# Moving z products, merge gates and the first scan in the order of a four-block fp32 kernel

## The chip, the cores and the metric

One core of one Trainium2 chip. The metric is the device time of one execution in microseconds. The times before are 3188.27, 3188.68 and 3191.09 us, median 3188.68.

## The reference

Two layers of a first block (retention, two convolution branches, a gated feed-forward part), then two layers of a second block, on 512 positions of width 1024 in float32. The change touches the second block alone. Cut to that:

```python
h = rmsnorm_2(x, pre_norm_g[l]); proj = h @ w_in[l]
u, v, z_a, c_q, c_kv, k_rope, z_b, x_c, z_c, g_a, g_b, g_c = split(proj)
y_a = gmlp_spatial(u, v, ...) * silu(z_a)
y_b = mla_attention(c_q, c_kv, k_rope, ...) * silu(z_b)      # 8 heads, softmax(q k^T) v
y_c = rg_lru(x_c, ...) * silu(z_c)                           # width 1280
merged = sigmoid(g_a) * (y_a @ w_proj_a[l]) + sigmoid(g_b) * (y_b @ w_proj_b[l]) \
       + sigmoid(g_c) * (y_c @ w_proj_c[l])
x = x + rmsnorm_2(merged @ w_out[l], post_norm_g[l])

# rg_lru: causal convolution of 4 taps, then
r = sigmoid(xb @ w_a + b_a); i = sigmoid(xb @ w_x + b_x)     # blocks of 80 channels
a = exp(-8 * r * softplus(-lam)); b = sqrt(max(1 - a * a, 0)) * (i * xc)
h[t] = a[t] * h[t-1] + b[t]                                  # the scan over positions
```

## The kernel before

Every large product is made in three passes: an operand x is split into a part that the fast fp32r format holds, hi (on ScalarE, lines 179, 307, 315), and the rest, lo = x - hi (on VectorE, lines 180, 308, 316), and `mm3` (lines 323 to 325) issues hi x hi, hi x lo and lo x hi. Channels lie on the 128 partitions, the 512 positions along the free dimension. A projection of 128 output channels from 1024 inputs (`projT`) is 8 blocks, so 24 matmuls of 512 columns.

The weights come from memory in one long stream, laid out in the order in which the program takes them. `Stream` loads them in pairs of chunks (1 MB, line 166, on SyncE's queue, two buffers), and splits a chunk of 1024 columns, 8 blocks, into hi and lo when the program comes within `AHEAD` = 4 chunks of it; `RING` = 7 split chunks fit. The split is issued at that point of the program, on ScalarE (line 179) and VectorE (line 180), so it stands in their queues behind all that was issued earlier.

The program is one hand-written order: each engine runs its instructions in the order in which the code issues them, and waits for the others by semaphores. Work that may be spread is put into a lane, a generator; `tick` runs one step of each lane, and `drain` the rest.

The second block (`block2`) runs `mla_down`, three z products of the B branch, the attention (`mla`), the merge of B, the recurrence (`lru`), the merge of C, the gMLP branch, the merge of A and the output projection. A z product is a `projT`, a sigmoid on ScalarE (line 942) and a product on VectorE (line 943).

In `mla`, `group(0)` makes the rotated parts of four heads' queries, then z(3), then head 0's projections and their split (`proj_split`, lines 315 and 316). For each head come the scores (from line 998), the next head's projections, the normalisation of the probabilities on VectorE (line 1016), then fillers from the table `FILL`: v a group of values, p the product with the values of the head before (`pv`, line 1048), g the second group of rotations, z a z product. At the end `out` transposes the probabilities on TensorE (line 1027). After head 7: z(7), then pv(7). In `merge` (B with two, C with four gates ahead) a gate is a `projT` and a sigmoid (line 673); output m is a product with all operands (line 684).

In `lru` there are ten tiles of 128 channels. A loop over m issues conv(m + 3), copies of rows between tiles by DMA (`pack`), a z product of C at m = 4, 6, 7, 8, and gates(m) (sigmoids line 1175, product line 1178). A scan (`scan`, a lane) is: two exponentials per tile on ScalarE (lines 1188, 1189), a small step on VectorE (line 1191), the square roots (line 1194), then per tile a product and the scan (lines 1197, 1198). The first scan has tiles 0 to 3 and is issued after gates(3), with two ticks per tile; it is drained before the second, of tiles 4 to 9, is issued behind the loop. A second loop issues the other six z products and, between them, multiplies finished operands (line 1239) and splits them, lo on POOL. The last two operands come behind that loop (line 1249).

Of the kernel before, what the change touches and what calls it, by code (L numbers as in the profile page):

```python
# [23 lines left out]
RING = 7  # L24
# [61 lines left out]
ZPOS = (4, 6, 7, 8)  # L86


FILL = ("v", "p", "gp", "p", "pv", "zp", "zp", "zp")
UNITS = 16  # L90


# [145 lines left out]
class Kernel:  # L238
# [709 lines left out]
    def mla(self, l, c, zb):  # L948

        nc, s, p = self.nc, self.s, self.p  # L950
# [5 lines left out]
        def group(g):  # L956
            pa = self.projT("mla_w_uq_2", l, ("qr", g, 0), op=c["cq"])
            pb = self.projT("mla_w_uq_2", l, ("qr", g, 1), op=c["cq"])
            x1, x2 = self.rotate(pa, pb, c["cos"], c["sin"])
            for i in range(4):  # L960
                grp["q", 4 * g + i] = self.stack(i, (x1.hi, x2.hi, x1.lo, x2.lo))
            return x1.hi, x1.lo, x2.hi, x2.lo
# [99 lines left out]
        def z(h):  # L1062

            t = self.z_silu(l, E_ZB + 128 * h)
            if h < len(zb):
                nc.vector.tensor_tensor(zb[h][:], zb[h][:], t[:], op=ALU.mult)
                s.f(t)
            else:
                zb.append(t)

        used = group(0)
        z(3)
        proj_split(0, *proj(0))
        for h in range(8):
            self.ws.ahead(self.ws.cur + AHEAD + 1)
            scores(h)
# [16 lines left out]
        s.f(c["cos"], c["sin"], c["kr"].hi, c["kr"].lo)  # L1093
        for o in c["cq"] + c["ckv"]:
            s.f(o.hi, o.lo)
        z(7)
        pv(7)
        for h in range(4):
            zb[h] = self.split(zb[h])

    def lru(self, l):
        nc, s, p = self.nc, self.s, self.p
        tt = nc.vector.tensor_tensor
        xc, op = {}, {}
        ws = self.ws

        lam = self.col("lam", l, 0, NLT)
        sp = self.sm.tile([128, 6 * NLT], F32, tag="sp", name="sp", bufs=1)
        a, b, c, d, sc1, sc2 = (sp[:, NLT * i:NLT * i + NLT] for i in range(6))
        ts = nc.vector.tensor_scalar  # L1110
        ts(a, lam, -1.0, 0.0, op0=ALU.mult, op1=ALU.max)
        ts(b, lam, 0.0, 2.0, op0=ALU.max, op1=ALU.mult)
        tt(b, lam, b, op=ALU.subtract)
        nc.scalar.activation(c, b, AF.Exp)
        nc.scalar.activation(d, c, AF.Ln, bias=1.0)
        tt(a, a, d, op=ALU.add)
        ts(sc1, a, -8.0, None, op0=ALU.mult)
        ts(sc2, a, -16.0, None, op0=ALU.mult)

        def conv(m):  # L1120
            ps = self.projT("w_in_2", l, E_XC + 128 * m)
            w = lambda k: self.col("lcw", l, 4 * m + k)
            t = s.t()
            nc.scalar.activation(t[:], ps[:], AF.Identity, bias=self.col("lcb", l, m), scale=w(3))
            for k in (2, 1, 0):
                sh = 3 - k
                nc.vector.scalar_tensor_tensor(t[:, sh:], ps[:, :S - sh], w(k), t[:, sh:], op0=ALU.mult, op1=ALU.add)
            p.f(ps)
            hi, lo = s.t(F32R), s.t(F32R)
            nc.scalar.activation(hi[:], t[:], AF.Copy)  # L1130
            tt(lo[:], t[:], hi.r(), op=ALU.subtract)
            xc[m], op[m] = t, Op(hi, lo)
            self.tick()

        rr, ii, pk = {}, {}, {}

        def pack(m):

            out = lru_outside(m)
            n = sum(r1 - r0 for _, r0, r1 in out)  # L1140
            one = 3 * n <= 128
            tiles = [s.t(F32R)] if one else [s.t(F32R), s.t(F32R)]
            for i, part in enumerate(("hi", "lo", "hi") if one else ("hi", "lo")):
                t, o = (tiles[0], n * i) if one else (tiles[i], 0)
                for k, r0, r1 in out:
                    eng = nc.sync if part == "lo" else nc.gpsimd
                    eng.dma_start(t[o:o + r1 - r0, :].bitcast(F32), getattr(op[k], part)[r0:r1, :].bitcast(F32))
                    o += r1 - r0
            pk[m] = (n, tiles)

        gw = {}

        def gate_weights(m):

            n = len(lru_rows(m))
            for nm in ("lru_w_a_2", "lru_w_x_2"):
                a = ws.take(128, (nm, l, 128 * m, 128 * m))
                hi, lo = ws.take(128, (nm, l, lru_rows(m), 128 * m))
                if n % 3 == 0 and n <= 96:
                    k = slice(n // 3 * 2, n)  # L1160
                    nc.gpsimd.tensor_copy(hi[k], lo[k].bitcast(F32))
                gw[nm, m] = (a, (hi, lo))

        def gates(m):
            n, tiles = pk.pop(m)
            for nm, bias, dst in (("lru_w_a_2", "lba", rr), ("lru_w_x_2", "lbx", ii)):
                a, (hi, lo) = gw.pop((nm, m))
                ps = p.t()
                self.mm3(ps[:], a, (op[m].hi[:], op[m].lo[:]), True, False)
                if len(tiles) == 1:  # L1170
                    nc.tensor.matmul(ps[:], hi[0:3 * n], tiles[0][0:3 * n, :], start=False, stop=True)
                else:
                    self.mm3(ps[:], (hi[0:n], lo[0:n]), (tiles[0][0:n, :], tiles[1][0:n, :]), False, True)
                t = s.t()
                nc.scalar.activation(t[:], ps[:], AF.Sigmoid, bias=self.col(bias, l, m))
                p.f(ps)
                dst[m] = t
            tt(ii[m][:], ii[m][:], xc[m][:], op=ALU.mult)
            o = op.pop(m)
            s.f(xc.pop(m), o.hi, o.lo, *tiles)  # L1180
            self.tick()

        h = {}

        def scan(ms):
            for m in ms:
                h[m] = s.t()
                nc.scalar.activation(h[m][:], rr[m][:], AF.Exp, scale=sc2[:, m:m + 1])  # L1188
                nc.scalar.activation(rr[m][:], rr[m][:], AF.Exp, scale=sc1[:, m:m + 1])  # L1189
            for m in ms:  # L1190
                ts(h[m][:], h[m][:], 1.0, 0.0, op0=ALU.subtract, op1=ALU.min)
            yield
            for m in ms:
                nc.scalar.activation(h[m][:], h[m][:], AF.Sqrt, scale=-1.0)  # L1194
            yield
            for m in ms:
                tt(ii[m][:], ii[m][:], h[m][:], op=ALU.mult)  # L1197
                nc.vector.tensor_tensor_scan(h[m][:], rr[m][:], ii[m][:], 0.0, op0=ALU.mult, op1=ALU.add)
                s.f(rr.pop(m), ii.pop(m))
                yield  # L1200
                if len(ms) == 4:
                    yield

        conv(0)
        conv(1)
        pack(0)
        conv(2)
        pack(1)
        pz, sz = {}, {}
        gate_weights(0)  # L1210
        for m in range(NLT):
            if m + 1 < NLT:
                gate_weights(m + 1)
            if m + 3 < NLT:
                conv(m + 3)
                pack(m + 2)
                if m + 3 == NLT - 1:
                    pack(NLT - 1)
            if m in ZPOS:
                z = len(sz) + len(pz)  # L1220
                ps = self.projT("w_in_2", l, E_ZC + 128 * z)
                if m < 8:
                    sz[z] = self.silu(ps)
                else:
                    pz[z] = ps
                self.tick()
            gates(m)
            if m == 3:
                self.lane("scan", scan(range(4)))
        self.drain("scan")  # L1230
        self.lane("scan", scan(range(4, NLT)))
        ops = []
        nz = len(sz) + len(pz)
        for z in range(nz, NLT):
            pz[z] = self.projT("w_in_2", l, E_ZC + 128 * z)
            self.tick()
            for m in range(len(ops), z - 1):
                t = sz.pop(m) if m in sz else self.silu(pz.pop(m))
                tt(t[:], t[:], h[m][:], op=ALU.mult)  # L1239
                s.f(h.pop(m))  # L1240
                ops.append(self.split(t, eng=nc.gpsimd))
                if m >= nz - 2:
                    break
            self.tick()
        self.drain("scan")
        rest = [self.silu(pz.pop(m)) for m in range(len(ops), NLT)]
        for t in rest:
            m = len(ops)
            tt(t[:], t[:], h[m][:], op=ALU.mult)
            s.f(h.pop(m))  # L1250
            ops.append(self.split(t))
        return ops
# [69 lines left out]
    def block2(self, l, last=False):  # L1322
        s = self.s
        c = self.mla_down(l)
        zb = []
# [5 lines left out]
            if h:  # L1331
                self.tick(3)
        self.drain("mla")
        self.mla(l, c, zb)

        def yb():
            return [z if isinstance(z, Op) else self.split(z) for z in zb]

        acc = {}
# [166 lines left out]
```

## Time and profile before

| | us |
|---|---|
| median of three runs | 3188.68 |
| the profiled execution | 3187.51 |
| its span, first to last instruction | 3185.7 |
| TensorE busy (mean granted clock 0.999) | 3139.7 (99%) |
| VectorE busy | 1862.8 (58%) |
| ScalarE busy | 1192.0 (37%) |
| POOL busy | 236.0 (7%) |

PE is TensorE, PEld its weight load, DVE VectorE, ACT ScalarE, SP SyncE. In a timeline a row has the start (us from the span's start), the length, the engine, the line, the operation, out<-in by the program's names without numbers (s a slot in SBUF, p a bank in PSUM, whi and wlo the split weights, hh and hl the split input), the shape and how many in a row; in brackets the engine's idle time ahead of it and what ended that. Matmuls overlap, so their pace is read from start to start. In the rows on stretches: the stretch and its length, the busy time of PE, PEld, DVE, ACT and POOL with (x instructions), the granted clock of TensorE, the share of the DMA engines, GB/s. The four blocks follow each other; the second block's two layers repeat the same pattern about 771 us apart (TensorE at 2057.09 and 2828.53).

### The profile page before, as it was taken

Reading aid. Unit: us, or ns where it says so; the run is one execution under the profiler, and the core shown is the slowest. Engines: PE = TensorE matmul, PEld = TensorE weight load, DVE = VectorE, ACT = ScalarE, POOL = GpSimd, SP = SyncE. Lnnn points to the kernel's source line nnn. Section 1 sums busy time; section 2 is a strip of 40 time slices with the busy share of each in tenths; the row PEclk is TensorE's granted clock in tenths of the full one; section 3 lists DMA queues with packets and bytes.
Section 4 is the critical chain, followed back from the end, with each engine's and each line's share of the span. In section 5 each row is a group of like instructions: output and inputs, shape, how many; then the busy total and the mean of one; then the engine's idle time right before and its main releaser. Section 6 shows DMA issues by size and latency. Waiting matters only on the chain. (4 is left out here: it accounts for less than half of the span.)

```text
span 3185.7 us, 36912 instructions
## 1 busy us (share of the span) xinstructions
PE 3139.7 (99%) x14808; PEld 2637.0 (83%) x14808; DVE 1862.8 (58%) x2727; ACT 1192.0 (37%) x1798; POOL 236.0 (7%) x364
## 2 busy tenths in 40 slices
PE   8999999999999999999999999999999999999998
PEld 7888888888888888888888888788888888878887
DVE  5687556663568755666448636735546854663643
ACT  4222343343322233333345525622225543642222
POOL 2000010000200000000011001200002000120000
PEclk9999999999999999999999999999999999999999
DMA  6222322232432232223323123332333223332232
GB/s 197 93 100 93 132 80 106 93 119 106 146 106 87 93 132 83 103 93 108 117 85 126 54 105 113 126 126 80 119 119 119 79 80 105 118 126 106 93 106 73
DMA packets 62539, 337.98 MB, mean 106 GB/s; under 512 B 10304, under 2 KB 10432, under 8 KB 27552
## 3 DMA queue, kind: packets, MB, share of 16 engines
q1 hardware_dynamic: 49984, 302.54, 26.8%
q0 software_dynamic: 11232, 31.08, 3.4%
q8 instruction: 116, 1.90, 0.2%
q10 hardware_dynamic: 1152, 2.01, 0.2%
q14 instruction: 55, 0.45, 0.0%
HBM read 310.68 MB, written 8.39 MB: 100 GB/s over the span
## 5 line engine op out<-in xcount | busy, mean ns | idle before, releaser
L323 PE MATMUL p<-hh,whi 128*128 128x512 f32 (+1 forms) x2752 | 1048.8, 381 | 1.6 <-ACT whi L179 1.6
L325 PE MATMUL p<-hh,wlo 128*128 128x512 f32 (+1 forms) x2752 | 1045.2, 380 | 1.5 <-DVE wlo L180 1.5
L324 PE MATMUL p<-hl,whi 128*128 128x512 f32 (+1 forms) x2752 | 1045.0, 380 | 0.0
L180 DVE TENSOR_TENSOR wlo<-raw,whi 128x1024 fp32r<-128x1024 f32 x544 | 671.7, 1242 | 476.7 <-ACT whi L179 475.5
L179 ACT ACTIVATE whi<-raw 128x1024 fp32r<-128x1024 f32 x544 | 563.2, 1052 | 313.5 <-PE p L325 189.1
L325 PEld LDWEIGHTS p<-hh,wlo 128*128 128x128 f32 x2752 | 518.6, 188 | 99.3 <-DVE wlo L180 1.8
L323 PEld LDWEIGHTS p<-hh,whi 128*128 128x128 f32 x2752 | 518.9, 189 | 98.5 <-ACT whi L179 2.0
L324 PEld LDWEIGHTS p<-hl,whi 128*128 128x128 f32 x2752 | 519.0, 189 | 96.1
L323 PE MATMUL p<-s,whi 128*128 128x512 f32 (+1 forms) x768 | 300.2, 391 | 3.1 <-ACT whi L179 2.6
L325 PE MATMUL p<-s,wlo 128*128 128x512 f32 (+1 forms) x768 | 299.2, 390 | 1.0 <-DVE wlo L180 1.0
L324 PE MATMUL p<-s,whi 128*128 128x512 f32 (+1 forms) x768 | 299.4, 390 | 0.4 <-DMA s<-s 0.4
L323 PE MATMUL p<-whi,s 128*128 128x512 f32 x640 | 250.1, 391 | 0.0
L325 PE MATMUL p<-whi,s 128*128 128x512 f32 x640 | 249.2, 389 | 0.0
L324 PE MATMUL p<-wlo,s 128*128 128x512 f32 x640 | 249.1, 389 | 0.0
L307 ACT ACTIVATE s<-s 128x512 fp32r<-128x512 f32 x168 | 103.4, 627 | 361.1 <-DVE s L689 129.4
L673 ACT ACTIVATE s<-p 128x512 f32<-128x512 f32 x96 | 57.3, 597 | 414.4 <-PE p L325 414.4
L813 DVE SCALAR_TENSOR_TENSOR s<-p,pv,s 128x511 f32<-128x511 f32 (+1 forms) x176 | 131.8, 749 | 122.3 <-ACT s L810 119.2
L684 DVE TENSOR_TENSOR s<-p,s 128x512 f32<-128x512 f32 x96 | 66.3, 690 | 194.2 <-PE p L325 194.2
L567 DVE SCALAR_TENSOR_TENSOR s<-s,pv,s 128x511 f32<-128x511 f32 (+14 forms) x240 | 176.0, 733 | 5.7
L323 PEld LDWEIGHTS p<-s,whi 128*128 128x128 f32 (+1 forms) x768 | 144.3, 188 | 34.1 <-ACT whi L179 3.5
L325 PEld LDWEIGHTS p<-s,wlo 128*128 128x128 f32 (+1 forms) x768 | 144.1, 188 | 32.0 <-DVE wlo L180 1.9
L324 PEld LDWEIGHTS p<-s,whi 128*128 128x128 f32 (+1 forms) x768 | 144.3, 188 | 30.3 <-DMA s<-s 0.5
(187 smaller groups left out, 3046.4 us busy)
## 6 DMA issues: line engine op xcount, KB each, us to landing
raw<-in_w_dram SPq DMA_DIRECT2D x272, 1024.0 KB, 4.8
s<-in_rows_dram POOLq DMA_DIRECT2D x32, 256.0 KB, 3.5
s<-s POOLq DMA_DIRECT2D x96, 64.0 KB, 2.6
xd<-s SPq DMA_DIRECT2D x24, 256.0 KB, 2.0
s<-xd POOLq DMA_DIRECT2D x24, 256.0 KB, 3.3
s<-s SPq DMA_DIRECT2D x88, 64.0 KB, 2.8
s<-in_cst_dram POOLq DMA_DIRECT2D x16, 256.0 KB, 3.6
s<-in_x_dram POOLq DMA_DIRECT2D x8, 256.0 KB, 5.5
```

The costliest lines, as they stand in the source:

```text
L179: nc.scalar.activation(hi[:], src, AF.Copy)
L180: nc.vector.tensor_tensor(lo[:], src, hi[:].bitcast(F32), op=ALU.subtract)
L307: self.nc.scalar.activation(hi[:, :n], t[:, :n], AF.Copy)
L323: mm(ps, a[0], b[0], start=first, stop=False)
L324: mm(ps, a[0], b[1], start=False, stop=False)
L325: mm(ps, a[1], b[0], start=False, stop=last)
L567: nc.vector.scalar_tensor_tensor(c[:, sh:], glu[:, :S - sh], w(k), c[:, sh:], op0=ALU.mult, op1=ALU.add)
L673: nc.scalar.activation(sgs[m][:], pg[:], AF.Sigmoid)
L684: nc.vector.tensor_tensor(sg[:], py[:], sg[:], op=ALU.mult)
L813: nc.vector.scalar_tensor_tensor(t[:, sh:], ps[:, :S - sh], w(k), t[:, sh:], op0=ALU.mult, op1=ALU.add)
```

## The change

Attention: z(3) goes behind head 0's projections, so ahead of the first scores; head 3 gets a z product ahead of pv(2), the later ones move up by one, and z(7), which stood behind head 7, becomes head 7's filler; pv(7) is returned as a function and runs in the merge of B behind its first two gates. Recurrence: the first scan is issued after gates(6) instead of gates(3), with one tick per tile instead of two, and isn't drained; the second scan follows in the same lane. The lo of all of C's operands is made on VectorE. Two more chunks are split ahead of the last two operands' products.

```diff
--- before.py
+++ after.py
@@ -86,7 +86,7 @@
 ZPOS = (4, 6, 7, 8)
 
 
-FILL = ("v", "p", "gp", "p", "pv", "zp", "zp", "zp")
+FILL = ("v", "p", "gp", "zp", "pv", "zp", "zp", "zp")
 UNITS = 16
 
 
@@ -1069,8 +1069,8 @@
                 zb.append(t)
 
         used = group(0)
+        proj_split(0, *proj(0))
         z(3)
-        proj_split(0, *proj(0))
         for h in range(8):
             self.ws.ahead(self.ws.cur + AHEAD + 1)
             scores(h)
@@ -1093,10 +1093,9 @@
         s.f(c["cos"], c["sin"], c["kr"].hi, c["kr"].lo)
         for o in c["cq"] + c["ckv"]:
             s.f(o.hi, o.lo)
-        z(7)
-        pv(7)
         for h in range(4):
             zb[h] = self.split(zb[h])
+        return lambda: pv(7)
 
     def lru(self, l):
         nc, s, p = self.nc, self.s, self.p
@@ -1198,8 +1197,6 @@
                 nc.vector.tensor_tensor_scan(h[m][:], rr[m][:], ii[m][:], 0.0, op0=ALU.mult, op1=ALU.add)
                 s.f(rr.pop(m), ii.pop(m))
                 yield
-                if len(ms) == 4:
-                    yield
 
         conv(0)
         conv(1)
@@ -1225,9 +1222,8 @@
                     pz[z] = ps
                 self.tick()
             gates(m)
-            if m == 3:
+            if m == 6:
                 self.lane("scan", scan(range(4)))
-        self.drain("scan")
         self.lane("scan", scan(range(4, NLT)))
         ops = []
         nz = len(sz) + len(pz)
@@ -1238,12 +1234,13 @@
                 t = sz.pop(m) if m in sz else self.silu(pz.pop(m))
                 tt(t[:], t[:], h[m][:], op=ALU.mult)
                 s.f(h.pop(m))
-                ops.append(self.split(t, eng=nc.gpsimd))
+                ops.append(self.split(t))
                 if m >= nz - 2:
                     break
             self.tick()
         self.drain("scan")
         rest = [self.silu(pz.pop(m)) for m in range(len(ops), NLT)]
+        self.ws.ahead(self.ws.cur + RING - 1)
         for t in rest:
             m = len(ops)
             tt(t[:], t[:], h[m][:], op=ALU.mult)
@@ -1331,9 +1328,10 @@
             if h:
                 self.tick(3)
         self.drain("mla")
-        self.mla(l, c, zb)
+        pv_last = self.mla(l, c, zb)
 
         def yb():
+            pv_last()
             return [z if isinstance(z, Op) else self.split(z) for z in zb]
 
         acc = {}
```

ScalarE, layer 0, around the second scan (L179 splits a weight chunk, L307 makes an operand's hi, L1188 in the kernel before and L1187 now is the scan's first exponential). Before:

```order
L179 ACTIVATE whi_15285<-raw_15167 128x1024
L1188 ACT_TABLE_LOAD
L1188 ACTIVATE s_981_15314<-s_957_14978,sp 128x512
L1189 ACTIVATE s_957_14978<-s_957_14978,sp 128x512
...
L1189 ACTIVATE s_979_15275<-s_979_15275,sp 128x512
L307 ACTIVATE s_987_15339<-s_956_14966 128x512
L307 ACTIVATE s_989_15344<-s_971_15139 128x512
L307 ACTIVATE s_991_15349<-s_974_15198 128x512
L1194 ACT_TABLE_LOAD
```

and now:

```order
L179 ACTIVATE whi_15283<-raw_15141 128x1024
L307 ACTIVATE s_981_15315<-s_952_14950 128x512
L307 ACTIVATE s_983_15320<-s_967_15115 128x512
L307 ACTIVATE s_985_15325<-s_970_15172 128x512
L1187 ACT_TABLE_LOAD
L1187 ACTIVATE s_987_15329<-s_953_14958,sp 128x512
L1188 ACTIVATE s_953_14958<-s_953_14958,sp 128x512
...
L1188 ACTIVATE s_979_15271<-s_979_15271,sp 128x512
L179 ACTIVATE whi_15353<-raw_15141 128x1024
L1193 ACT_TABLE_LOAD
```

The three operands' hi splits stood behind the second scan's exponentials and stand ahead of them now; a weight split that stood ahead of the exponentials is followed by one that now stands behind them.

VectorE at the same place (L1191/L1190 is the step behind the exponential, L1196/L1197 and L1197/L1198 the product and the scan of a tile, L1239/L1235 the product that makes an operand, L308 its lo split). Before:

```order
L1191 TENSOR_SCALAR s_986_15329<-s_986_15329 128x512
L1239 TENSOR_TENSOR s_956_14966<-s_956_14966,s_950_14915 128x512
L1239 TENSOR_TENSOR s_971_15139<-s_971_15139,s_951_14918 128x512
L1239 TENSOR_TENSOR s_974_15198<-s_974_15198,s_952_14921 128x512
L180 TENSOR_TENSOR wlo_15360<-raw_15167,whi_15359 128x1024
L1197 TENSOR_TENSOR s_958_14985<-s_958_14985,s_981_15314 128x512
L1198 SCALAR_TENSOR_TENSOR s_981_15314<-s_957_14978,s_958_14985 128x512
```

and now:

```order
L180 TENSOR_TENSOR wlo_15284<-raw_15141,whi_15283 128x1024
L1196 TENSOR_TENSOR s_946_14870<-s_946_14870,s_974_15184 128x512
L1197 SCALAR_TENSOR_TENSOR s_974_15184<-s_945_14861,s_946_14870 128x512
L1235 TENSOR_TENSOR s_952_14950<-s_952_14950,s_971_15175 128x512
L308 TENSOR_TENSOR s_982_15316<-s_952_14950,s_981_15315 128x512
L1235 TENSOR_TENSOR s_967_15115<-s_967_15115,s_972_15178 128x512
L308 TENSOR_TENSOR s_984_15321<-s_967_15115,s_983_15320 128x512
L1235 TENSOR_TENSOR s_970_15172<-s_970_15172,s_973_15181 128x512
L308 TENSOR_TENSOR s_986_15326<-s_970_15172,s_985_15325 128x512
L1190 TENSOR_SCALAR s_987_15329<-s_987_15329 128x512
```

The last tile of the first scan stands directly ahead of the operands now, and each operand's lo split follows its product on VectorE; the second scan's first steps come behind all of them.

ScalarE behind C's last z product (L942 the sigmoids of the last two, L673 the first merge gate). Before:

```order
L942 ACTIVATE s_1008_15562<-p_561_15490 128x512
L942 ACTIVATE s_1009_15565<-p_562_15529 128x512
L307 ACTIVATE s_1010_15569<-s_1008_15562 128x512
L307 ACTIVATE s_1012_15574<-s_1009_15565 128x512
L179 ACTIVATE whi_15578<-raw_15447 128x1024
L673 ACTIVATE s_1014_15607<-p_563_15582 128x512
```

and now:

```order
L942 ACTIVATE s_1008_15562<-p_561_15488 128x512
L942 ACTIVATE s_1009_15565<-p_562_15529 128x512
L179 ACTIVATE whi_15568<-raw_15445 128x1024
L179 ACTIVATE whi_15572<-raw_15445 128x1024
L307 ACTIVATE s_1010_15579<-s_1008_15562 128x512
L307 ACTIVATE s_1012_15584<-s_1009_15565 128x512
L673 ACTIVATE s_1014_15613<-p_563_15588 128x512
```

Two weight chunks, of which one was behind the operands' splits, are split ahead of them.

## Rows read from the trace of the kernel before

**Rows 1.** Page, section 1: busy us (share of span) x instructions, by engine.
```profile
PE 3139.7 (99%) x14808; PEld 2637.0 (83%) x14808; DVE 1862.8 (58%) x2727; ACT 1192.0 (37%) x1798; POOL 236.0 (7%) x364
```

**Rows 2.** TensorE's timeline, layer 0's attention: start us, length us, instruction [idle, releaser].
```profile
1701.51 0.39 PE L325 MATMUL p<-s,wlo 128*128 128x512 f32 x1
...
1703.31 0.50 PE L999 MATMUL p<-s,s 128*128 128x512 f32 x1 [0.23 <-DVE s L316]
...
1747.88 0.38 PE L1048 MATMUL p<-s,s 128*128 128x128 f32 x2
1749.59 0.30 PE L1027 MATMUL p<-ident,s 128*128 128x128 f32 x1 [1.33 <-DVE s L1016]
```

**Rows 3.** TensorE's timeline, layer 0's recurrence and the head of the C merge.
```profile
1988.78 0.39 PE L323 MATMUL p<-s,whi 128*128 128x512 f32 x1
...
1996.54 0.39 PE L325 MATMUL p<-s,wlo 128*128 128x512 f32 x1
...
1998.00 0.40 PE L325 MATMUL p<-s,wlo 112*128 112x512 f32 x1
...
2001.47 0.43 PE L323 MATMUL p<-hh,whi 128*128 128x512 f32 x1
...
2057.09 0.39 PE L325 MATMUL p<-s,wlo 128*128 128x512 f32 x1
...
2059.62 0.50 PE L325 MATMUL p<-s,wlo 128*128 128x512 f32 x1 [0.52 <-DVE wlo L180]
```

**Rows 4.** TensorE's timeline, the same place of layer 1.
```profile
2828.53 0.39 PE L325 MATMUL p<-s,wlo 128*128 128x512 f32 x1
...
2831.93 0.50 PE L325 MATMUL p<-s,wlo 128*128 128x512 f32 x1 [0.52 <-DVE wlo L180]
```

**Rows 5.** ScalarE's timeline, layer 0, first scan.
```profile
1961.70 1.28 ACT L1188 ACT_TABLE_LOAD   x1
...
1968.49 1.05 ACT L179 ACTIVATE whi<-raw 128x1024 fp32r<-128x1024 f32 x1
...
1971.47 1.28 ACT L1194 ACT_TABLE_LOAD   x1
...
1974.98 1.28 ACT L1175 ACT_TABLE_LOAD   x1
1976.27 1.27 ACT L1175 ACTIVATE s<-p,pv 128x512 f32<-128x512 f32 x2
```

**Rows 6.** ScalarE's timeline, layer 0, second scan.
```profile
2005.57 1.28 ACT L1188 ACT_TABLE_LOAD   x1
...
2015.54 1.84 ACT L307 ACTIVATE s<-s 128x512 fp32r<-128x512 f32 x3 [0.34 <-DVE s L1239]
...
2024.18 0.60 ACT L942 ACTIVATE s<-p 128x512 f32<-128x512 f32 x1
```

**Rows 7.** VectorE's timeline, layer 0, second scan to C merge.
```profile
2022.90 1.23 DVE L180 TENSOR_TENSOR wlo<-raw,whi 128x1024 fp32r<-128x1024 f32 x1 [6.20 <-ACT whi L179]
2024.05 0.68 DVE L1197 TENSOR_TENSOR s<-s,s 128x512 f32<-128x512 f32 x1
...
2025.91 0.67 DVE L943 TENSOR_TENSOR s<-p,s 128x512 f32<-128x512 f32 x1
2026.61 0.69 DVE L1239 TENSOR_TENSOR s<-s,s 128x512 f32<-128x512 f32 x1
...
2029.08 2.25 DVE L180 TENSOR_TENSOR wlo<-raw,whi 128x1024 fp32r<-128x1024 f32 x1
...
2053.95 0.68 DVE L1249 TENSOR_TENSOR s<-s,s 128x512 f32<-128x512 f32 x1
...
2056.01 0.69 DVE L1249 TENSOR_TENSOR s<-s,s 128x512 f32<-128x512 f32 x1
2057.40 0.69 DVE L308 TENSOR_TENSOR s<-s,s 128x512 fp32r<-128x512 f32 x1 [0.70 <-ACT s L307]
```

**Rows 8.** Busy us by engine in 5 us near the end; PEclk: granted clock.
```profile
3180.00:3185.00 5.00, 0.00 (x0) 0.00 (x0) 0.00 (x0) 0.00 (x0) 0.00 (x0) 0.50 0.03 11
```

## The prediction

> **What bounds the kernel now.** I read the page first. TensorE is busy 99% of the span, VectorE 58%, ScalarE 37% [rows 1], so the change, which leaves the number of matmuls as it is, can only move the stretches in which TensorE stands still. Then TensorE's own instructions where the edits lie, by their starts: a matmul of 512 columns starts 0.227 us after the one before (245 of them between the starts at 2001.47 and 2057.09, 55.62 us [rows 3]), so a larger step is lost time. Last come the queues of ScalarE and VectorE in the recurrence, because each runs in program order: whatever stands ahead of a weight split there holds it up.
>
> The steps that the change can take back, in layer 0:
> - First scores: from 1701.51 to 1703.31, two steps, 1.80 us, so 1.34 lost, behind the split of head 0's q and k on ScalarE [rows 2].
> - Head 3's transposes: from the last matmul of pv(2) (two from 1747.88) to 1749.59, 1.71 us for two matmuls of 128 columns, some 0.11 each by the step of 512, so 1.5 lost to the normalisation on VectorE [rows 2].
> - Gates of the ninth tile: 1996.54 to 1998.00, three steps, 1.46 us, so 0.78 lost to a copy that comes late [rows 3].
> - First product of the C merge: 2057.09 to 2059.62, three steps, 2.53 us, so 1.85 lost to the two halves of one weight chunk [rows 3]; in layer 1, 2828.53 to 2831.93, so 2.72 [rows 4].
> The attention ones I count alike in layer 1. All of it together: 2 x (1.34 + 1.5 + 0.78) + 1.85 + 2.72 = 11.8 us, 0.37% of the span. That is about the most that the change can give.
>
> **The attention part.** z(3) now stands between proj(0) and the first scores. Its 24 matmuls, 24 x 0.227 = 5.4 us, cover q's and k's splits, of which the trace shows 1.34 us uncovered; the rotation's results stay as far ahead of the scores as they were, since the same three products lie between. I take 1.34 back. At head 3 another product of 5.4 us lies ahead of pv(2) and covers the 1.5. Its sigmoid adds two table loads of 1.28 us each [rows 5] per layer on ScalarE; head 4's long filler (pv(3) and the second group of values) hides them, and if it did not, they would cost at most 2.6 us per layer. pv(7) behind two gates loses its own wait; what is late next is operand 7 of the merge, which needs a product and four splits on VectorE, some 0.7 us each, 3.5 us, and is used 21 matmuls, 4.8 us, after pv(7). I cost it at nothing; without that cover it is at most 3.5 us per layer. SP carries as many loads as before, in the same order against the copies. Sum: -2 x (1.34 + 1.5) = -5.7 us.
>
> **The recurrence part** decides. Before, the first scan is issued after gates(3). Its exponentials, table loads and four scans delay the last convolutions, which is why the ninth gates wait. Now it is issued after gates(6): that wait goes, 2 x 0.78 = 1.6 us. But the first scan's chain then starts only when TensorE has finished the z product of tile 7, at 1988.78 [rows 3], and the second scan queues behind it. In layer 0's time, from rows:
> - The sigmoid of that z product, 0.6 [rows 6], some 0.2 behind it: 1989.6. Table and eight exponentials: 1961.70 to 1968.49, 6.8; table and two sigmoids 2.5; table and four roots 1971.47 to 1974.98, 3.5; the weight split behind them 1.05 [rows 5]. ScalarE is at 2003.4.
> - VectorE must take that chunk's lo half first, 1.15; then four tiles at 1.86 (a product and a scan: 2024.05 to 2025.91), two gate products of about 0.7 between them, one more chunk 1.15 [rows 7]: 2014.65.
> - Three operands. Now VectorE makes the lo split, not POOL, and each round of product, ScalarE's hi, lo takes 2.06 (2053.95 to 2056.01 [rows 7]). The third hi ends after two rounds and 1.4: 2020.1. ScalarE's three hi splits stand **ahead** of the second scan's exponentials; before they stood behind them. So these start at 2020.1 and not at 2005.57 [rows 6].
> - From that table load to the end of the sigmoid of C's fourth z product it took 19.2 us (2005.57 to 2024.78), of which 2.2 were the three hi splits and the wait for them [rows 6]: now 17.0, so 2037.1, 12.3 us later than before.
> - VectorE's queue from there to the last operand: five rounds of silu product and split, 0.70 + 2.06 = 2.76 each, 13.8; six tiles 11.2; six chunks 6.9; two silu products 1.4; two last rounds 4.1. Sum 37.4: the last lo half is ready at 2074.5; before, it was at 2058.09 [rows 7].
> TensorE without a wait would start the merge's first product six z products and four gates, 240 matmuls, after 2001.47 - 0.78 = 2000.69, at 2055.2, and need that last half 28 matmuls on, at 2061.5. It waits 13.0 us in all, not at one place: the chunk for the last z product comes some 2 us late, the one for the first merge gate some 5 us, the next two 2 to 3 each. Against that, the wait of 1.85 and 2.72 us at this place is gone, which is contained in the 13.0.
>
> The lo splits on VectorE are not the loss: beside POOL's split a chunk's lo half took 2.25 us, without it 1.23 [rows 7], so 0.7 more work buys back 1.0. The two chunks split ahead of the last silu products help only at the very end, when the earlier chunks have already been late.
>
> **Sum:** 2 x 13.0 - 11.8 = **+14.2 us**. The profiled execution took 3187.5 us (span 3185.7), so 3201.7; the median of the runs shown is 1.2 above it, so 3202.9. Most roundings in the queues went up; I say 3202.
>
> Bounds: the 13.0 is a chain of waits, each with one row behind it. If the gate products cost 0.6 and ScalarE's hi splits hide better, it is 11; if a raw weight load lands late once per layer, as before the second scan's table load, it is 15. That is 3198 to 3207.
>
> **The rivals.**
> 1. *The ring's cover holds: faster.* Weights are split four chunks, 22 us, ahead. Before, VectorE's second chunk after the roots was done at 2031.3 [rows 7] and TensorE needed it in the merge's first gate, at 2001.47 + 150 x 0.227 = 2035.5: 4 us to spare. If the second scan comes less than 4 us later than now, the lag costs nothing, the late chunk goes too, and the whole 11.8 comes back: 3188.7 - 11.8 = 3177. For it speaks that the ring hides a lag now: the chunk whose lo half ran at 2022.90 [rows 7] was issued with the product that TensorE began at 2001.47 + 24 x 0.227 = 2006.9, 16 us earlier. Against it speaks the order of the three hi splits, which adds 12.3.
> 2. *Half of the lag is hidden: no change.* The break-even is a wait of 5.9 us per layer where I have 13.0. It would need the four scans or the three rounds to run beside the exponentials, which the order of either queue forbids as I read it.
> 3. *TensorE's clock.* [...] A wait of 5 us is new, and the clock may fall in it. If the next 24 matmuls ran at half speed, they would take 5.4 us more, but 2 to 3 us of that goes into each of the next two waits, since VectorE's queue sets the end: nothing, or next to it. If 48 did, 10.9 us less some 6 of waits would stay, 5 us per layer: 3202 + 10 = 3212. [...] The rows at the end of the trace agree that it falls; no row shows how fast it comes back.
>
> **How the numbers follow.** My forecast has 0.76, the cover that holds 0.08, the half-hidden lag 0.08, the clock's hard form 0.08. Of the forecast's own chance nearly all lies in 3195 to 3208. With the lower part of the clock's case and the upper part of the half-hidden one, 8 in 10 lie in 3192 to 3211. A difference of 0.2%, 6.4 us, is about what a measurement of this kernel can tell from none. Slower by more: the forecast and the clock, 0.83, with a hundredth off for a forecast that ends low; the same 0.09; faster 0.08.
>
> **What would show it.** Right, step by step: no wait at the first scores (L998) or at head 3's transposes; none at the ninth gates; the second scan's table load at some 2017 in layer 0 (2020.1 less the 3 us gained ahead of it), behind three hi splits; TensorE waiting for ScalarE and VectorE's weight splits, four or five times, 11 to 15 us per layer, the longest in the first gate of the C merge; busy TensorE time as before. Wrong: the second scan's table load before 2010, or those waits under 6 us per layer. If they are there and the time is still 3189, I have missed a gain elsewhere.

## The result and the profile after

The changed kernel takes 3210.51 us (median of 4 runs, 3207.7 to 3212.59), the kernel before 3189.89 (4 runs, 3188.27 to 3192.11): a ratio of 1.0064, 95% interval 1.0052 to 1.0076. It is slower by 20.6 us. Its profiled execution took 3207.7 us (span 3205.9, against 3185.7). Further below, one of ten runs of one kernel took 7963.14 us at a granted clock of 0.445; it is in no median.

Section 1 of the page after, which answers to [rows 1]:

```profile
PE 3149.3 (98%) x14808; PEld 2645.0 (83%) x14808; DVE 1868.3 (58%) x2743; ACT 1197.3 (37%) x1802; POOL 208.8 (7%) x348
```

TensorE has as many matmuls and is busy 9.6 us longer (some of them run at a lower clock, below); the rest of the 20.2 us of span is time in which it stands still. Its waits, in the view of waits of the kernel after (line that waits <- line waited for: us in all, times, longest):

```profile
PE p L416 <- DVE s L400: 17.3, 11, 10.8
PE p L323 <- ACT whi L179: 12.1, 5, 3.7
PE p L325 <- DVE wlo L180: 9.6, 9, 2.0
PE p L324 <- DVE wlo L180: 4.6, 3, 1.9
PE p L927 <- ACT s L878: 2.0, 2, 1.6
```

The waits of the attention (L998, L999, L1027) and for a copy are gone. What grew are the waits for split weights, whi from ScalarE and wlo from VectorE. TensorE's timeline after shows where:

```profile
1704.03 0.39 PE L998 MATMUL p<-s,s 128*128 128x512 f32 x1
1704.26 0.39 PE L999 MATMUL p<-s,s 128*128 128x512 f32 x1
...
1754.12 0.38 PE L1048 MATMUL p<-s,s 128*128 128x128 f32 x2
1754.34 1.26 PE L1027 MATMUL p<-ident,s 128*128 128x128 f32 x10
...
2027.65 0.39 PE L325 MATMUL p<-hh,wlo 128*128 128x512 f32 x1
2031.76 0.50 PE L323 MATMUL p<-hh,whi 128*128 128x512 f32 x1 [3.73 <-ACT whi L179]
...
2033.02 0.80 PE L325 MATMUL p<-hh,wlo 128*128 128x512 f32 x1 [0.53 <-DVE wlo L180]
2033.62 0.63 PE L323 MATMUL p<-hh,whi 128*128 128x512 f32 x1
2034.04 0.63 PE L324 MATMUL p<-hl,whi 128*128 128x512 f32 x1
...
2041.26 0.50 PE L323 MATMUL p<-hh,whi 128*128 128x512 f32 x1 [1.62 <-ACT whi L179]
...
2044.02 0.80 PE L325 MATMUL p<-hh,wlo 128*128 128x512 f32 x1 [2.02 <-DVE wlo L180]
...
2059.09 0.50 PE L325 MATMUL p<-hh,wlo 128*128 128x512 f32 x1 [1.31 <-DVE wlo L180]
...
2065.12 0.50 PE L325 MATMUL p<-hh,wlo 128*128 128x512 f32 x1 [0.31 <-DVE wlo L180]
```

The two places of [rows 2] are seamless now: the scores follow at 0.23, the transposes at 0.22 behind pv(2). Against that stand six waits at the end of the recurrence, 9.5 us in all, in the last z product of C and in the gates of its merge; layer 1 has six at the same places, 9.1 us. Another 3.9 us, by their steps, are matmuls at the lower clock. From 2033.62 to 2034.04 a matmul takes 0.42 instead of 0.227: the clock is down, at 0.50 in the two microseconds from 2033 to 2035. The stretches of the kernel after there (us; busy us of PE, PEld, DVE, ACT, POOL; granted clock; DMA share; GB/s):

```profile
2026.00:2032.00 6.00, 2.27 (x10) 1.58 (x10) 1.91 (x5) 5.89 (x9) 0.00 (x0) 1.00 0.00 0
2032.00:2038.00 6.00, 5.47 (x18) 4.10 (x18) 0.97 (x1) 5.97 (x9) 0.00 (x0) 0.72 0.50 175
2038.00:2044.00 6.00, 2.37 (x10) 1.32 (x8) 5.05 (x7) 2.21 (x4) 0.00 (x0) 0.90 0.01 1
2044.00:2050.00 6.00, 5.98 (x15) 4.74 (x16) 5.20 (x7) 2.06 (x3) 0.00 (x0) 0.53 0.01 3
2050.00:2056.00 6.00, 6.00 (x28) 4.97 (x27) 5.23 (x8) 1.30 (x2) 0.00 (x0) 1.00 0.51 175
```

ScalarE after, which answers to [rows 5, 6]:

```profile
1989.43 1.06 ACT L179 ACTIVATE whi<-raw 128x1024 fp32r<-128x1024 f32 x1 [5.25 <-PE p L1170]
1990.39 0.58 ACT L942 ACTIVATE s<-p 128x512 f32<-128x512 f32 x1
1990.99 1.28 ACT L1187 ACT_TABLE_LOAD   x1
...
2016.52 0.63 ACT L307 ACTIVATE s<-s 128x512 fp32r<-128x512 f32 x1 [6.92 <-DVE s L1235]
2018.51 0.63 ACT L307 ACTIVATE s<-s 128x512 fp32r<-128x512 f32 x1 [1.36 <-DVE s L1235]
2020.50 0.63 ACT L307 ACTIVATE s<-s 128x512 fp32r<-128x512 f32 x1 [1.36 <-DVE s L1235]
2021.15 1.28 ACT L1187 ACT_TABLE_LOAD   x1
...
2037.55 0.60 ACT L942 ACTIVATE s<-p 128x512 f32<-128x512 f32 x1
```

The second scan's table load is behind the three hi splits, at 2021.15 where it was at 2005.57. In the 11.6 us ahead of it, from 2009.6 on, ScalarE stands idle for 9.64 (6.92 and twice 1.36) while TensorE runs towards weights that are not yet split. In the kernel before, the three products that stand there followed each other on VectorE without a lo split between them:

```profile
2014.82 1.89 DVE L1239 TENSOR_TENSOR s<-s,s 128x512 f32<-128x512 f32 x3
```

VectorE after, which answers to [rows 7]:

```profile
2015.82 0.67 DVE L1235 TENSOR_TENSOR s<-s,s 128x512 f32<-128x512 f32 x1
2017.18 0.69 DVE L308 TENSOR_TENSOR s<-s,s 128x512 fp32r<-128x512 f32 x1 [0.70 <-ACT s L307]
2017.79 0.68 DVE L1235 TENSOR_TENSOR s<-s,s 128x512 f32<-128x512 f32 x1
...
2038.18 0.69 DVE L943 TENSOR_TENSOR s<-p,s 128x512 f32<-128x512 f32 x1 [5.21 <-ACT s L942]
...
2042.76 1.20 DVE L180 TENSOR_TENSOR wlo<-raw,whi 128x1024 fp32r<-128x1024 f32 x1
...
2050.30 1.20 DVE L180 TENSOR_TENSOR wlo<-raw,whi 128x1024 fp32r<-128x1024 f32 x1
...
2074.68 0.69 DVE L308 TENSOR_TENSOR s<-s,s 128x512 fp32r<-128x512 f32 x1 [0.70 <-ACT s L307]
```

A round of product, hi and lo takes 1.97 us, in which VectorE waits 0.70 for ScalarE's hi. From 2038.18 on VectorE has hardly any idle time but these 0.7, and its first three weight chunks come 7.54 us apart.

**Where the 20.2 us of span went.** The n-th matmul of the program is the same point of the work in both traces as long as the order around it is the same. So the start after less the start before, the shift, read ahead of and behind each part, gives the part's price:

| part | layer 0 | layer 1 |
|---|---|---|
| ahead of the second block's downward projection | -0.7 | |
| downward projection (`mla_down`, not changed) | +3.0 | +1.1 |
| attention | -3.7 | -3.7 |
| ninth gates | -0.8 | -1.2 |
| last z products to the end of the C merge | +13.5 | +12.7 |

Together 20.2. The rest of the text calls the last part the tail. In the trace of the recurrence part alone (second experiment below) the tails cost 13.6 and 12.7; `mla_down`, whose code is the same in all kernels, comes out anywhere from 0.0 to 5.4 per layer in the ten traces behind the one before, so its row is scatter.

### The profile page after: what moved, and what is told of

Its sections match the earlier page's. It is cut to its first block, busy times and chain, and to the rows that moved or that the text cites. A ratio compares the mean times of both kernels' runs of the same rounds, so it can differ in the third digit from the quotient of the medians.

```text
span 3205.9 us, 36895 instructions
## 1 busy us (share of the span) xinstructions
PE 3149.3 (98%) x14808; PEld 2645.0 (83%) x14808; DVE 1868.3 (58%) x2743; ACT 1197.3 (37%) x1802; POOL 208.8 (7%) x348
## 5 line engine op out<-in xcount | busy, mean ns | idle before, releaser
L179 ACT ACTIVATE whi<-raw 128x1024 fp32r<-128x1024 f32 x544 | 563.5, 1052 | 330.7 <-PE p L325 188.8
L323 PEld LDWEIGHTS p<-hh,whi 128*128 128x128 f32 x2752 | 520.8, 189 | 110.6 <-ACT whi L179 14.2
L307 ACT ACTIVATE s<-s 128x512 fp32r<-128x512 f32 x168 | 103.7, 627 | 384.6 <-DVE s L689 129.4
L673 ACT ACTIVATE s<-p 128x512 f32<-128x512 f32 x96 | 57.1, 597 | 409.2 <-PE p L325 409.2
```

Source lines behind the costliest of these rows:

```text
L179: nc.scalar.activation(hi[:], src, AF.Copy)
L307: self.nc.scalar.activation(hi[:, :n], t[:, :n], AF.Copy)
L323: mm(ps, a[0], b[0], start=first, stop=False)
L673: nc.scalar.activation(sgs[m][:], pg[:], AF.Sigmoid)
```

## The experiments

Theory A is the prediction's: the order of ScalarE's queue, with the first scan begun late and three hi splits ahead of the second scan's exponentials, makes the tail long. Its rivals are TensorE's clock and other parts of the same edit: the lo split on VectorE, the late first scan without the hi splits. Diffs are against the kernel named; line numbers shift by a few between the kernels.

**The attention part alone** (before, with the edits to `FILL`, z(3) and pv(7)).

> The kernel before with the attention part alone (z(3) behind head 0's projections, head 3's filler, pv(7) behind two gates). Theory A (the recurrence's queues lose the time, the attention part gains): the starts of TensorE's matmuls in the changed kernel are 3.8 us nearer per layer at the end of the attention, so 3189.9 - 7.6 = 3182, and the recurrence's waits are those of the kernel before (0.8 to 1.1 us at the ninth gates, 1.9 and 2.7 at the C merge). Theory B (the attention part costs something later): 3190 or more.

Measured: 3183.33 us (10 runs) against 3190.01, ratio 0.9979 (0.9970 to 0.9989). 6.7 us faster; its part of the change does what it was costed at.

**The recurrence part alone** (before, with the other edits).

> The kernel before with the recurrence part alone (first scan behind gates(6), not drained, lo of C's operands on VectorE, two chunks split early). Theory A: the loss stays whole: 3189.9 + 2 x 12.2 = 3214 (the changed kernel's shift from the ninth gates to the C merge's first product is 12.6 in layer 0 and 11.4 in layer 1), second scan's table load some 32 us behind the end of tile 7's z product. Theory B: the loss is under 12 us, the rest came from the attention part.

Measured: 3214.7 us (4 runs), ratio 1.0077 (1.0062 to 1.0092). The whole loss is in this part. Its trace keeps the attention's waits and has the tail's, as its view of waits says:

```profile
PE p L323 <- ACT whi L179: 12.2, 5, 3.7
PE p L325 <- DVE wlo L180: 9.5, 9, 2.0
...
PE p L1027 <- DVE s L1016: 2.7, 2, 1.3
PE p L998 <- ACT s L315: 1.4, 2, 0.7
```

**The lo splits back on POOL, all else changed:**

```diff
-                ops.append(self.split(t))
+                ops.append(self.split(t, eng=nc.gpsimd))
```

> The changed kernel with the lo of C's operands on POOL again. Theory A (the three hi splits ahead of the second scan's exponentials, and the first scan begun late): the three rounds on VectorE shrink from 2.0 to 0.7 us each, so the exponentials start 2.6 us earlier; VectorE's tail loses five lo splits and their waits (6.8 us) and gets back 4 slow weight splits (4 x 1.0): the last operand some 5 us earlier per layer, 3210.5 - 10 = 3200, still 10 us above the kernel before. Theory C (VectorE was overloaded by the moved lo splits, and the order matters little): about 3185, with no wait in the first merge gate.

Measured: 3201.77 us (5 runs), ratio 1.0036 (1.0023 to 1.0049). More than half of the loss stays, as A said; but 8.7 us went with the lo splits (7.0 in the two tails), where the prediction had said that they are not the loss.

**The exponentials first.** One tick more ahead of the three operands puts the second scan's exponentials ahead of their hi splits again, the rest as changed:

```diff
-            self.tick()
+            self.tick(2 if z == nz else 1)
             for m in range(len(ops), z - 1):
```

> The changed kernel with one tick more ahead of the first three operands, so that the second scan's exponentials stand ahead of their hi splits on ScalarE as in the kernel before; lo stays on VectorE. Theory A: the table load starts at about 2010 instead of 2021 in layer 0's time; the three rounds of 2.0 us and the roots follow, the sigmoid of C's fourth z product ends at about 2032 instead of 2038, and the last operand comes 6 us earlier per layer: 3210.5 - 12 = 3198. Theory C: VectorE's queue is as long as before, so 3208 to 3211.

Measured: 3194.39 us (10 runs), ratio 1.0013 (1.0003 to 1.0022). A single tick takes back 16.1 of the 20.6 us. By the shifts the two tails give 12.8 of it, about the 12 that A had expected; the rest isn't theirs (the two traces differ by 2.8 in `mla_down`, which the tick doesn't touch). ScalarE's timeline of this kernel:

```profile
2007.60 1.28 ACT L1187 ACT_TABLE_LOAD   x1
...
2017.57 0.63 ACT L307 ACTIVATE s<-s 128x512 fp32r<-128x512 f32 x1 [0.34 <-DVE s L1235]
...
2029.00 0.60 ACT L942 ACTIVATE s<-p 128x512 f32<-128x512 f32 x1
```

The table load is at 2007.60 instead of 2021.15, where TensorE is 2.0 us earlier (shifts -4.26 and -2.24), so 11.5 us of that is the order; and the first hi split behind the exponentials waits 0.34 instead of 6.92: the idle time that ScalarE had ahead of the exponentials now holds them.

**The first scan back in its place** (before, with the attention part, lo on VectorE and the two early chunks).

> The changed kernel with the scan where it was (first scan behind gates(3), two ticks a tile, drained): what is left is the attention part, lo on VectorE and the two early chunks. Theory A: the second scan's table load is back at about 2005 of layer 0's time less the attention's gain; the three rounds of product, hi, lo still take 2.0 us each ahead of the roots, so C's fourth sigmoid ends 3 to 4 us later than in the kernel before and the last operand some 3 us after TensorE could use it: 3 us of waits per layer, 3187. If lo on VectorE costs nothing, as the prediction said of it: 3181.

Measured: 3184.49 us (10 runs), ratio 0.9982 (0.9972 to 0.9991): midway between the two; the price of the lo splits is read two experiments on.

**The two early chunks alone:**

```diff
         rest = [self.silu(pz.pop(m)) for m in range(len(ops), NLT)]
+        self.ws.ahead(self.ws.cur + RING - 1)
```

> The kernel before with the two chunks split ahead of the last operands' products alone. If the wait at the C merge's first product (1.85 and 2.72 us) is the order of that weight split behind the operands, both go: 3190.0 - 4.6 = 3185.4. If the operands themselves are as late, the wait moves to them and the time stays 3190.

Measured: 3186.59 us (10 runs), ratio 0.9984 (0.9974 to 0.9993) against 3190.45. In the trace the first product of the C merge waits no more; the shift falls there by 1.98 in layer 0 and 2.85 in layer 1. This piece is a gain by itself.

**Attention and early chunks, nothing else.**

> The kernel before with the attention part and the two early chunks, the recurrence's scan and POOL's lo as before. Theory A: the attention part alone took 6.7 us off, and its profile shows 1.35 and 1.30 us of waits left at the C merge's first product; without these 3183.3 - 2.6 = 3180.7, the fastest of all. If the operands are late instead: 3183.

Measured: 3178.29 us (4 runs, 3177.47 to 3182.06), ratio 0.9963 (0.9948 to 0.9978). It beats both kernels: 12.2 us under before, 32.2 under the changed one. Beside the kernel with the first scan back, from which it differs in the lo splits' engine alone, it prices them: 3184.49 - 3178.29 = 6.2 us (5.6 in the two tails). VectorE's timeline with lo on POOL (this kernel):

```profile
2026.81 2.25 DVE L180 TENSOR_TENSOR wlo<-raw,whi 128x1024 fp32r<-128x1024 f32 x1
...
2034.00 2.25 DVE L180 TENSOR_TENSOR wlo<-raw,whi 128x1024 fp32r<-128x1024 f32 x1
```

POOL's in the same kernel:

```profile
2025.77 2.20 POOL L308 TENSOR_TENSOR s<-s,s 128x512 fp32r<-128x512 f32 x1 [7.68 <-ACT s L307]
```

And VectorE's with lo on VectorE (the kernel with the first scan back):

```profile
2030.14 1.20 DVE L180 TENSOR_TENSOR wlo<-raw,whi 128x1024 fp32r<-128x1024 f32 x1
...
2037.68 1.20 DVE L180 TENSOR_TENSOR wlo<-raw,whi 128x1024 fp32r<-128x1024 f32 x1
```

Beside POOL the weight split takes 2.25 instead of 1.20, and yet the chunks come every 7.19 us with POOL and every 7.54 without. VectorE's split is 1.05 longer where POOL's ran 1.16 into it; why, the rows don't show. By the length of the weight split alone the move to VectorE gains; the chunks' pace says that it loses.

**Exponentials first and lo on POOL:** what is left of the recurrence part is the late first scan and the early chunks.

> The changed kernel with the second scan's exponentials ahead of the three operands and lo on POOL: of the changed recurrence only the late first scan is left. Theory A: exponentials at about 2010, hi splits right behind them, roots done at about 2025, C's fourth sigmoid at 2027, the last operand at about 2062, 1 us after it could be used: 3182 to 3184. If the late first scan is the loss by itself: 3194 or more, as with lo on VectorE.

Measured: 3187.23 us (9 runs), ratio 0.9989 (0.9979 to 0.9998): between the two expectations. Against the kernel with attention and early chunks alone, 3178.29, the late first scan (with its single ticks and without its drain) costs 8.9 us by itself.

**One weight split behind the first scan's exponentials.** In the trace after, a split stands ahead of the first scan and waits 5.25 us for a ring buffer (first row of ScalarE's timeline above). Here it is issued behind the exponentials, all else as changed (while `lazy` is set, the stream splits no chunk ahead of the one in use; code between the two places is left out):

```diff
+                self.ws.lazy = m == 7
                 ps = self.projT("w_in_2", l, E_ZC + 128 * z)
+                self.ws.lazy = False
...
                 self.tick()
+                if m == 7:
+                    self.ws.ahead(self.ws.cur + AHEAD)
```

> The changed kernel, with the one weight split that stands ahead of the first scan on ScalarE (in the trace it waits 5.25 us for a ring buffer that the gates of tile 7 still read, and the sigmoid of the z product behind it starts at 1990.39 instead of some 1987.5) issued behind the scan's eight exponentials. Theory A (this wait is what the prediction left out of the first scan's chain): that sigmoid starts 2.9 us earlier, the split itself, 1.06, still stands in the chain, so the second scan's table load comes 1.8 us earlier, at some 2019.3 in layer 0, and each layer's recurrence is 1.8 us shorter: 3210.5 - 3.7 = 3206.8. Rival B (the chain waits for something else as well, the gates' results or the slots): table load where it was, 3210.5.

Measured: 3204.94 us (5 runs), ratio 1.0045 (1.0031 to 1.0059). ScalarE's timeline of this kernel:

```profile
1985.75 0.60 ACT L942 ACTIVATE s<-p 128x512 f32<-128x512 f32 x1 [3.40 <-PE p L325]
1986.37 1.28 ACT L1187 ACT_TABLE_LOAD   x1
...
2017.48 1.28 ACT L1187 ACT_TABLE_LOAD   x1
...
2033.89 0.60 ACT L942 ACTIVATE s<-p 128x512 f32<-128x512 f32 x1
```

The sigmoid now waits for its z product alone. TensorE is 1.83 us earlier at this place than in the profile after (shifts -3.23 and -1.40), so the sigmoid gained 1990.39 - 1985.75 - 1.83 = 2.8 us, and the second table load 2021.15 - 2017.48 - 1.83 = 1.84, as A had it. The tail became 1.8 us shorter in both layers, 3.6 in all; A had expected 3.7.

**One number for all of them.** VectorE's queue in the tail starts behind the sigmoid of C's fourth z product (line 942 behind the second scan's roots). Its lag is its start less the 2024.18 of [rows 6], less TensorE's shift just ahead of the tail. Beside it stands what the tail cost in layer 0, with the 1.98 that the early chunks give back added where they are in:

| kernel | sigmoid's start | TensorE's shift | lag | tail's cost |
|---|---|---|---|---|
| attention alone | 2022.71 | -1.41 | -0.1 | 0.0 |
| first scan back | 2023.86 | -3.12 | 2.8 | 2.8 |
| exponentials first, lo on POOL | 2026.11 | -4.36 | 6.3 | 5.3 |
| exponentials first | 2029.00 | -4.26 | 9.1 | 9.1 |
| lo on POOL | 2033.99 | -3.05 | 12.9 | 12.0 |
| split behind the exponentials | 2033.89 | -4.07 | 13.8 | 13.7 |
| recurrence alone | 2041.30 | +1.51 | 15.6 | 15.5 |
| changed kernel | 2037.55 | -2.24 | 15.6 | 15.5 |

In eight kernels the tail of layer 0 costs what this one sigmoid is late, all of it with lo on VectorE, and all but 0.8 to 1.0 with lo on POOL. In layer 1 (2.85 added) the cost is 0.8 to 0.9 above the lag in the five kernels with lo on VectorE and a lag, from 1.9 and 2.8 (first scan back) to 14.7 and 15.5 (changed kernel): the same slope from another zero.

## Why the prediction was right in direction, and where its steps failed

The forecast, 3202, is 8.5 us too low; the measured 3210.51 lies just inside the range of 3192 to 3211, and above the bounds of 3198 to 3207 that the sum itself was given.

- **Attention: right, mis-sized.** The two waits went. The term was -5.7; the shifts give 3.7 + 3.7 = 7.4. Left out were the scores behind head 3's transposes, which had a step of 0.59 (1750.89 to 1751.48 in the trace before) and have one of 0.32 now, and smaller ones.
- **Ninth gates: right.** 0.78 per layer forecast, 0.8 and 1.2 measured.
- **The first scan's chain: the step that failed.** "The sigmoid of that z product, 0.6 [rows 6], some 0.2 behind it: 1989.6." TensorE ended that product 1.4 us earlier than before, so this became 1988.2; the sigmoid ended at 1990.97. A weight split stands ahead of it in ScalarE's queue and waits for the ring buffer that the gates of tile 7 release. The last experiment shows it: 2.8 us. The prediction's sign, the second table load at some 2017, failed by 4.2 (2021.15): by this wait, and because only 1.4 of the 3 us that it took off for gains ahead were there where the chain begins. From there on the chain was right: to the end of the sigmoid of C's fourth z product 17.0 us forecast, 2021.15 to 2038.15 measured; VectorE's queue from there 37.4 forecast, to the end of the last lo at 2075.37, so 37.2.
- **The tail.** Forecast 13.0 less the C merge's 1.85 and 2.72 [rows 3, 4], so 11.1 and 10.3; measured 13.5 and 12.7. The 2.4 missing in each are the sigmoid's 2.8, but for the small differences. The waits lie about where they were expected, but the longest is that of the last z product (3.7 for 2), not that of the first gate, and the later ones are shorter, because slow matmuls stand in their place. So the waits alone come to 9.5 us and not to 11 to 15, and TensorE's busy time is not as before but 9.6 longer.
- **"The lo splits on VectorE are not the loss": wrong.** They cost 6.2 us by themselves, and 7.0 in the two tails of the changed kernel. The step compared work (0.7 against 1.0 us) and left out the 0.7 that VectorE waits for ScalarE's hi in every round. Three rounds take 6.0 us where three products together took 1.89, and each later chunk is 0.35 later.
- **Rival 1, the cover of 4 us: not for the chunks behind the first.** The first chunk did have 4 us to spare. But chunks came every 7.19 us and TensorE uses one in 24 x 0.227 = 5.45: 1.7 less for each, and the kernel with lo on POOL and a lag of 6.3 shows 1.0 in all. So the half-hidden lag of rival 2 had nothing to hide behind either.
- **Rival 3, the clock: held in its mild form,** the one of 24 slow matmuls that the next waits make up for. It fell to 0.50 (from 2033 to 2035 and from 2043 to 2049; means of 0.72 and 0.53 in the stretches above), and by their steps the slow matmuls lose 3.9 us, where that form had 5.4. What the slow matmuls lose is made up in the next waits, which are still 1.62 behind the first slow stretch and 1.31 and 0.31 behind the second: VectorE's queue set the end. The table of lags says the same, since the lag alone gives the cost: the kernel with the first scan back has a granted clock of 1.00 in every stretch from 2026 to 2056 and lies on the same line.
- **Not foreseen:** 3.0 and 1.1 us in `mla_down`, which the change doesn't touch (below). That is scatter; without it the result would have come nearer to the forecast.

Sum of the misses against the forecast of +14.2: tail 26.2 - 21.4 = +4.8, attention -1.7, ninth gates -0.4, `mla_down` +4.1, ahead of it -0.7. But for the rounding that is 6.0, and 14.2 + 6.0 = 20.2, the difference of the two spans. The other 2.5 of the 8.5 are no part of the mechanism: the profiled execution is 2.8 under its median where 1.2 was allowed for, and 3202.9 was put down as 3202.

## What to carry to other kernels

In engines that run in program order, look for the instruction behind which the split weights (or any shared supply) queue, and forecast its start relative to the consumer: here each microsecond of lag cost about a microsecond per layer. A ring that seems 4 us ahead has no such cover once its refill is slower than its use (here 7.19 us a chunk against 5.45); compare the pace of both over the whole stretch, not the margin of the first chunk. When work moves from one engine to another, count the waits of the ping-pong that it creates, not only the busy times.

## What the runs showed of the hardware that was not expected

The clock fell after waits shorter than the 5 us that the prediction asked about, and not each time. In `mla_down` of layer 0 TensorE has the same two waits for split weights in both traces, 1.86 and 0.92 us in the trace before, 1.87 and 0.91 in the one after. The stretch that follows, before:

```profile
1643.00:1647.00 4.00, 3.08 (x18) 2.76 (x18) 3.96 (x5) 2.81 (x7) 0.48 (x1) 1.00 0.31 76
```

and after:

```profile
1643.00:1647.00 4.00, 3.09 (x10) 3.09 (x11) 3.32 (x6) 2.31 (x8) 0.56 (x1) 0.57 0.51 123
```

The granted clock is 1.00 in the one and 0.57 in the other, and 10 matmuls lie in the stretch where 18 did. Of six experiments, three show the fall in this stretch too (attention alone 0.65, recurrence alone 0.57, attention and early chunks 0.57) and three don't (first scan back, exponentials first and split behind the exponentials, each 1.00), in kernels whose code up to there is the same. In the trace after it costs 1.3 us: the shift is -0.70 at the second wait's end (1644.61 and 1643.91) and +0.61 at the next transposes (L416, 1650.34 and 1650.95). A wait for ScalarE that follows (L927) takes 1.6 us in the trace after; the one before has none. What decides it was not tried. It is a part of the scatter between executions: a difference of 3 us between two single profiles of this program says nothing about an edit.
